# A fixed engine order for the first stage and the convolution of a hybrid recurrent/convolution decoder step, with later evictions and a gate pair moved to the end

## The chip, the cores and the metric

The kernel runs on one core of one Trainium2 chip. The metric is the device time in microseconds (us) of one execution; lower is better. A core has a matrix engine (PE, with its weight loads shown apart as PEld), a vector engine (DVE), an activation engine (ACT), a general engine (POOL) and a sync engine (SP), whose queue issues most DMAs. Each engine takes its own instructions in order and waits on semaphores for the others. [...]

## The reference, cut to what matters

One layer of a decoder: 16 learned meta tokens and 1,024 prompt tokens in one sequence, and 8 sequences of one token each ("samples") with a carried state. D_MODEL is 1,024.

```python
xn   = rmsnorm(h, norm_pre)
q, fr, i_in, z_a, b_g, c_g, h_c, z_b, gate_a, gate_b = split(xn @ w_in, 10)   # 1024 columns each
f    = lb + (1 - lb) * sigmoid(fr)                    # 8 heads of 128
S_t  = diag(f_t) S_{t-1} + (1 - f_t) i_t^T ;  o_t = silu(q_t)^T S_t
y_a  = (rmsnorm(o) * hgrn_norm * silu(z_a)) @ w_a
u    = c_g * h_c ;  conv = causal depthwise width-3 convolution of u
y_b  = (b_g * conv * silu(z_b)) @ w_b
out  = (sigmoid(gate_a) * y_a + sigmoid(gate_b) * y_b) @ w_o
h    = h + rmsnorm(out, norm_post)
```

It returns the prompt's and the samples' outputs, the new recurrent states and the new convolution contexts, all float32.

## The kernel before

Every float32 operand of a product is split into a high part (`fp32r`) and a low remainder, by `split`: a copy on ACT, then a subtraction on DVE or POOL. A product is three matmuls (`mm3`, lines 126 to 128).

**First stage.** Eight chunks of 128 tokens come in (even ones over SP's queue, odd ones in reversed order by an indirect DMA on POOL's queue). `prep_chunk` normalises a chunk (`normalise`: square with a row sum on ACT, inverse root on POOL, scaling on DVE at L186) and turns it (`turn`: four transposes on PE into a PSUM bank, high part on ACT, low part on DVE). The turned chunks are the column sets `b11, b21, b12, b22` of a two-by-two Strassen-like scheme with seven products; `sums12` and `sums34` (L207) form three more sets. Meanwhile `plain` computes the first head's `i` and `f` projections directly: four calls, each with 24 matmuls into one bank for `i` and 24 into another for `f`. Five masks for the recurrence (L82 to L88) are made at the very start.

**The stream.** `strassen` then computes all other projections in 39 pairs of sections. A pair has seven products (j = 0 to 6), each in two column chunks (c = 0, 1): 14 steps of 12 matmuls. In the step of product i, ACT makes the high part of the weights of product i + 2 (L687), DVE or POOL the low part (L693), and POOL the weight sums of the next pair (L673 to L675, L697). Right after its matmuls a step emits the eviction of its own output: for j = 0, 2, 4 a copy into a `held` tile (`sc`, L734), otherwise `evac`, which adds the held part (L270) and goes on with sigmoid and product. Some follow-up work goes into a list `later`, which `flush` empties in the next step.

**What is woven in.** `weave` spreads side work over the steps: the other turned sets over pair 0 (`later_sets`), then one head of the recurrence (`hgrn`) over every three pairs, then the eight samples' state updates (`sample_steps`) over the last fourteen pairs. Those pairs compute the convolution: `u_pair` forms u and its taps (L806, L808), `b_pair` multiplies by b and silu(z_b) (L828, L833, L834). Gate pairs (`gate_pair`) store sigmoid gates to DRAM; seven of them stand between the heads' pairs and the eighth stands right before the first `u_pair`. While the last pair runs, `fill` loads the heads' outputs back (`oz`, L925) and splits them.

**After the stream** `y_gemm` forms y_a and y_b (16 products of 96 matmuls each), the output projection follows, and the results are stored.

The order in which each engine gets its instructions is chosen by the scheduler of the language, by priorities in the order of the program and its own estimate of the times:

```python
for m in range(8):
    weave(stream, 42, hgrn(m), W_HG)
qz = slot("kt", 256)
pool.memset(qz, 0.0)
weave(stream, 14 * 14, sample_steps(), [1] * 64)
drain(stream)
context_out()
```

PSUM has two banks `ga`, two `gb` and four `h`. Weight operands (`w`) have three buffers, `sc` and `cs` two each. In odd pairs from number 25 on, a pair takes `h` banks in place of `ga`.

Of the kernel before, what the change touches and what calls it, by code (L numbers as in the profile page):

```python
# [19 lines left out]
HL = 524  # L20
# [12 lines left out]
def hybrid_step(ctx: ExitStack, tc: tile.TileContext,  # L33
# [46 lines left out]
    masks = const.tile([128, 5, 4, 128], U8, name="masks")  # L80
    pi, fi = slot("sc", 128, I32), slot("sc", 128, I32)
    pool.iota(pi[:, 0:128], pattern=[[0, 128]], base=0, channel_multiplier=1)  # L82
    pool.iota(fi[:, 0:128], pattern=[[1, 128]], base=0, channel_multiplier=0)
    for l in range(5):
        if l:
            for t in (pi, fi):
                vec.tensor_scalar(out=t[:, 0:128], in0=t[:, 0:128], scalar1=1, scalar2=None, op0=ALU.logical_shift_right)
        vec.tensor_tensor(out=masks[:, l], in0=cap(pi, 0, [[0, 4], [1, 128]]), in1=cap(fi, 0, [[0, 4], [1, 128]]),  # L88
                          op=ALU.is_equal)


# [71 lines left out]

    b11, b21, t2, b12, t3, t4, b22 = (factor(j) for j in range(7))
# [15 lines left out]
    def normalise(rows, xt):  # L180
        ms = small(1)
        act.activation(out=scratch[0:rows], in_=xt[0:rows, 0:1024], func=AF.Square, scale=1.0 / 32.0,
                       accum_out=ms[0:rows])
        rs = small(1)
        rsqrt(rs[0:rows], ms[0:rows])
        vec.scalar_tensor_tensor(out=xt[0:rows, 0:1024], in0=xt[0:rows, 0:1024], scalar=rs[0:rows, 0:1],  # L186
                                 in1=wpre[0:rows], op0=ALU.mult, op1=ALU.mult)

    def turn(xt, kk, to, c0):

        pt = hbank()
        for k in range(4):
            pe.transpose(pt[:, 128 * k:128 * k + 128], xt[:, 512 * kk + 128 * k:512 * kk + 128 * k + 128], ident)
        here = [[HL, 4], [1, 128]]
        split(cap(pt, 0, [[128, 4], [1, 128]]), cap(to[0], c0, here), cap(to[1], c0, here))

    def prep_chunk(c):
        xt = norm[c]
        normalise(128, xt)
        for kk in range(2):  # L200
            turn(xt, kk, ((b11, b12), (b21, b22))[kk][c % 2], 128 * (c // 2))
# [8 lines left out]
    def sums12(i, e1=None, e2=None):  # L210
        c = 2 * i
        less(block(c + 1, 0), block(c + 1, 0), block(c, 0), e1 or pool)
        less(block(c + 1, 1), block(c + 1, 1), block(c + 1, 0), e2 or vec)

    def sums34(i, e1=None, e2=None):
        c = 2 * i
        less(block(c, 0), block(c + 1, 1), block(c, 0), e1 or pool)
        less(block(c, 1), block(c, 1), block(c + 1, 1), e2 or pool)


    def load_small():
        xt = slot("k", 1024)
        sync.dma_start(xt[0:16, 0:1024], meta_tokens)
        sync.dma_start(xt[16:24, 0:1024], xs)
        return xt

    def prep_small(xt):

        normalise(24, xt)
        B = slot("sm", 192)  # L230
        for kk in range(2):
            pt = hbank()
            for k in range(4):
                c0 = 512 * kk + 128 * k
                pe.transpose(pt[:, 24 * k:24 * k + 24], xt[0:24, c0:c0 + 128], ident[0:24, 0:24])
# [18 lines left out]
    later = []  # L254

# [21 lines left out]

    def i_out(m, h, c0, n, pt, s):
# [6 lines left out]
    def f_out(m, h, c0, n, pt, s):  # L285
        out = of_head(m, "f", h, c0, n)
        sigmoid(added(pt, s, out), n, out)
        act.activation(out=out, in_=out, func=AF.Identity, scale=omlb[:, m:m + 1], bias=lb[:, m:m + 1])

    def q_out(m, h, c0, n, pt, s):  # L290
        out = of_head(m, "x", h, c0, n)
        y = added(pt, s)
        sg = sigmoid(y, n)
        later.append(lambda: (vec if s is None else pool).tensor_tensor(out=out, in0=y, in1=sg, op=ALU.mult))

    def z_out(m, h, c0, n, pt, s):
        out = of_head(m, "zs", h, c0, n)
        y = added(pt, s)
        sg = sigmoid(y, n)
        later.append(lambda: vec.scalar_tensor_tensor(out=out, in0=y, scalar=hnorm, in1=sg, op0=ALU.mult, op1=ALU.mult))  # L300
# [4 lines left out]
    def hgrn(m):  # L305
# [15 lines left out]
        turned(iT, V, 0)  # L321
# [7 lines left out]
        turned(iT, V, 1)  # L329
# [4 lines left out]
        ex = slot("ex", 24)  # L334
        pool.tensor_copy(cap(ex, 0, [[12, 2], [1, 12]]), cap(iT, 512, [[HL, 2], [1, 12]]))
# [192 lines left out]

    load_chunk(0)
    sync.dma_start(wpre, norm_pre.broadcast_to([128, 1024]))  # L530
    load_chunk(2)

    pv = slot("sm", 512)
    sync.dma_start(pv[0:16, 0:128], lb_logits.rearrange("j (m c) -> (j m) c", c=128))
    sync.dma_start(pv[16:40, 0:128], conv_w[0].rearrange("j (m c) -> (j m) c", c=128))
    sync.dma_start(pv[40:41, 0:128], hgrn_norm)
    pvp = hbank()
    pe.transpose(pvp[:, 0:41], pv[0:41, 0:128], ident[0:41, 0:41])
    vecs = const.tile([128, 41], F32, name="vecs")
    act.copy(vecs, pvp[:, 0:41])  # L540
    hnorm = vecs[:, 40:41]

    def tap(j, m):
        return vecs[:, 16 + 8 * j + m:17 + 8 * j + m]

    lbt = const.tile([128, 4, 8], F32, name="lbt")
    lb, omlb, mx, e1 = lbt[:, 0], lbt[:, 1], lbt[:, 2], lbt[:, 3]
    vec.tensor_tensor(out=mx, in0=vecs[:, 0:8], in1=vecs[:, 8:16], op=ALU.max)
    vec.tensor_tensor(out=lb, in0=vecs[:, 0:8], in1=mx, op=ALU.subtract)
    vec.tensor_tensor(out=e1, in0=vecs[:, 8:16], in1=mx, op=ALU.subtract)  # L550
    act.activation(out=lb, in_=lb, func=AF.Exp)
    act.activation(out=e1, in_=e1, func=AF.Exp)
    vec.tensor_tensor(out=e1, in0=e1, in1=lb, op=ALU.add)
    vec.reciprocal(out=e1, in_=e1)
    vec.tensor_tensor(out=lb, in0=lb, in1=e1, op=ALU.mult)
    vec.tensor_scalar(out=omlb, in0=lb, scalar1=-1.0, scalar2=1.0, op0=ALU.mult, op1=ALU.add)


    wp = (t4[0][:, 0:1024], t4[1][:, 0:1024])

    def plain(h, c0, n):

        banks = abank()[:, 0:n], bbank()[:, 0:n]
        for (wh, wl), pt in zip((wi, wf), banks):
            for k in range(8):
                xh, xl = at(((b11, b12), (b21, b22))[k // 4][h], k % 4)
                ks = slice(128 * k, 128 * k + 128)
                mm3(pt, wh[:, ks], wl[:, ks], xh[:, c0:c0 + n], xl[:, c0:c0 + n], k == 0, k == 7)

        def rest():  # L570
            for out, pt in zip((i_out, f_out), banks):
                out(0, h, c0, n, pt, None)
        return rest

    def part(to, which, i):
        turn(norm[2 * i + (which in (1, 2))], which in (2, 4), to, 128 * i)

    C0, C1 = chunks_of(HL)
    wi = weight(sec_of(2, 0), eng=pool)
    prep_chunk(0)  # L580
    load_chunk(1)
    prep_chunk(2)
    wf = weight(sec_of(1, 0), eng=pool, places=wp)
    load_chunk(3)
    for c in (4, 6):
        load_chunk(c)
    xsmall = load_small()
    for c in (5, 7):
        load_chunk(c)
    done = plain(0, *C0)  # L590
    prep_chunk(1)
    prep_chunk(3)
    done()
    done = plain(1, *C0)
    prep_chunk(4)
    prep_chunk(6)
    blocks = prep_small(xsmall)
    for b, to in zip(blocks, (b11, b12, b21, b22)):
        small_parts(b, to)
    done()  # L600
    sums12(0)
    sums12(1)
    part(t2, 2, 0)
    done = plain(0, *C1)
    prep_chunk(5)
    prep_chunk(7)
    s11, s12, s21, s22 = blocks
    for out, a, b, to in ((s12, s12, s11, None), (s22, s22, s12, t2), (s11, s22, s11, t3), (s21, s21, s22, None)):
        less(out, a, b, vec)
        if to:  # L610
            small_parts(out, to)
    done()
    part(t2, 2, 1)
    sums12(2)
    sums12(3)
    done = plain(1, *C1)
    part(t2, 2, 2)
    part(t2, 2, 3)
    for i in range(4):
        sums34(i)  # L620
    done()
    factors = [b11, b21, t2, b12, t3, t4, b22]

    def later_sets():

        part(b12, 1, 0)
        part(b12, 1, 1)
        small_parts(s12, b12)
        yield
        part(b12, 1, 2)  # L630
        part(b12, 1, 3)
        yield
        for i in range(4):
            part(t3, 3, i)
            if i % 2:
                yield
        small_parts(s21, t4)
        for i in range(4):
            part(t4, 4, i)
            if i % 2:  # L640
                yield
        cp = hbank()
        for h in range(2):
            cst = slot("sc", 512)
# [496 lines left out]
```

## Time and profile before

| | |
|---|---|
| time, median of 3 runs | 1313.67 us (1311.47 to 1315.06) |
| profiled execution | 1312.9 us, span 1311.1 us, mean granted clock 0.989 |
| PE busy | 1255.3 us (96%), 10,041 matmuls |
| DVE busy | 821.3 us (63%) |
| ACT busy | 538.0 us (41%) |
| POOL busy | 467.1 us (36%) |
| DMA | 117.12 MB, mean 89 GB/s |
| chain that ended last | PE 87%, POOL 5%, DVE 3%, DMA 2%, issue 2%, ACT 1% |

The span runs from the first to the last instruction; the profiled execution's own time is 1.8 us longer. "Granted clock" is the share of TensorE's full clock that the chip granted.

### The profile page before, as it was taken

Reading aid. Unit: us, or ns where it says so; the run is one execution under the profiler, and the core shown is the slowest. Engines: PE = TensorE matmul, PEld = TensorE weight load, DVE = VectorE, ACT = ScalarE, POOL = GpSimd, SP = SyncE. Lnnn points to the kernel's source line nnn. Section 1 sums busy time; section 2 is a strip of 40 time slices with the busy share of each in tenths; the row PEclk is TensorE's granted clock in tenths of the full one; section 3 lists DMA queues with packets and bytes.
Section 4 is the critical chain, followed back from the end, with each engine's and each line's share of the span. In section 5 each row is a group of like instructions: output and inputs, shape, how many; then the busy total and the mean of one; then the engine's idle time right before and its main releaser. Section 6 shows DMA issues by size and latency. Waiting matters only on the chain.

```text
span 1311.1 us, 25317 instructions
## 1 busy us (share of the span) xinstructions
PE 1255.3 (96%) x10041; PEld 1221.7 (93%) x10041; DVE 821.3 (63%) x1397; ACT 538.0 (41%) x1271; POOL 467.1 (36%) x530
## 2 busy tenths in 40 slices
PE   3799999999999999999999989989999999999997
PEld 3799999999999999999999889989999999999876
DVE  7558587785958678595876654755667623546052
ACT  5355555555555545555543333323334402313031
POOL 7555243333434333443344444653554000000010
PEclk9899999999999999999999999999999999999999
DMA  7011212121121212112214333332334633532041
GB/s 220 1 43 57 68 57 82 52 73 59 57 67 58 82 58 71 55 58 67 86 54 155 91 104 113 108 103 89 114 112 162 205 97 100 176 96 84 16 163 56
DMA packets 146533, 117.12 MB, mean 89 GB/s; under 512 B 6657, under 2 KB 130666, under 8 KB 146414
## 3 DMA queue, kind: packets, MB, share of 16 engines
q1 hardware_dynamic: 145838, 113.40, 27.7%
q0 software_dynamic: 576, 2.10, 0.5%
q8 instruction: 79, 1.29, 0.4%
q14 instruction: 40, 0.33, 0.1%
HBM read 89.48 MB, written 25.96 MB: 88 GB/s over the span
## 4 chain that ended last, share of the span: by engine, by line
PE 87%; POOL 5%; DVE 3%; DMA 2%; issue 2%; ACT 1%; DVEq 0%; SPq 0%; POOLq 0%; ACTq 0%
PE gb L126 10%; PE ga L127 10%; PE gb L127 10%; PE ga L126 10%; PE gb L128 10%; PE ga L128 10%; PE h L126 5%; PE h L128 5%; PE h L127 5%; PE h L413 3%; PE h L458 1%; PE h L318 1%; PE h L481 1%; PE h L479 1%; POOL ee L877 1%
## 5 line engine op out<-in xcount | busy, mean ns | idle before, releaser
L693 DVE TENSOR_TENSOR w<-wq,w 128x512 fp32r<-128x512 f32 x153 | 119.8, 783 | 68.3 <-ACT w L687 67.0
L687 ACT CAST w<-sm 128x512 fp32r<-128x512 f32 x117 | 72.3, 618 | 159.9 <-PE gb L128 128.3
L693 DVE TENSOR_TENSOR w<-sm,w 128x512 fp32r<-128x512 f32 x117 | 92.2, 788 | 36.5 <-ACT w L687 35.1
L734 ACT COPY sc<-ga 128x256 f32<-128x256 f32 x192 | 70.5, 371 | 89.3 <-PE ga L128 82.1
L1054 POOL TENSOR_TENSOR st<-st,half 128x1 f32<-128x1 f32 (+1 forms) x9 | 5.0, 551 | 279.3 <-DVE st L1052 276.4
L687 ACT CAST w<-wq 128x512 fp32r<-128x512 f32 x156 | 96.9, 621 | 16.8 <-PE h L128 13.2
L126 PE MATMUL gb<-s3h,w 128*128 128x256 f32 (+3 forms) x328 | 95.6, 291 | 6.5 <-DVE sc L270 5.7
L126 PE MATMUL gb<-s1h,w 128*128 128x256 f32 (+3 forms) x344 | 99.6, 290 | 0.0
L126 PE MATMUL gb<-s6h,w 128*128 128x256 f32 (+3 forms) x328 | 95.6, 292 | 1.6 <-DVE it L784 1.6
L127 PE MATMUL gb<-s1l,w 128*128 128x256 f32 (+3 forms) x344 | 97.2, 282 | 0.0
L127 PE MATMUL gb<-s6l,w 128*128 128x256 f32 (+3 forms) x328 | 93.7, 286 | 0.0
L127 PE MATMUL gb<-s3l,w 128*128 128x256 f32 (+3 forms) x328 | 93.7, 286 | 0.0
L128 PE MATMUL gb<-s3h,w 128*128 128x256 f32 (+3 forms) x312 | 89.2, 286 | 0.9 <-DVE w L693 0.9
L128 PE MATMUL gb<-s6h,w 128*128 128x256 f32 (+3 forms) x312 | 88.7, 284 | 0.0
L128 PE MATMUL gb<-s1h,w 128*128 128x256 f32 (+3 forms) x312 | 88.0, 282 | 0.0
L126 PE MATMUL ga<-s0h,w 128*128 128x256 f32 (+2 forms) x296 | 85.9, 290 | 0.0
L697 POOL TENSOR_TENSOR sm<-wq,sm 128x512 f32<-128x512 f32 x39 | 57.3, 1470 | 79.0 <-DVE w L693 58.7
L127 PE MATMUL ga<-s0l,w 128*128 128x256 f32 (+2 forms) x296 | 84.1, 284 | 0.6 <-DVE s0l L103 0.6
L126 PE MATMUL ga<-s5h,w 128*128 128x256 f32 (+3 forms) x256 | 74.5, 291 | 8.8 <-ACT sc L734 8.8
L126 PE MATMUL ga<-s2h,w 128*128 128x256 f32 (+3 forms) x272 | 79.8, 293 | 0.0
L675 POOL TENSOR_TENSOR sm<-wq 128x512 f32<-128x512 f32 x39 | 52.8, 1353 | 75.2 <-DVE w L693 74.3
L270 DVE TENSOR_TENSOR sc<-gb,sc 128x256 f32<-128x256 f32 (+1 forms) x144 | 60.4, 421 | 28.8 <-PE gb L128 16.7
(726 smaller groups left out, 4715.8 us busy)
## 6 DMA issues: line engine op xcount, KB each, us to landing
wq<-in_w_in_dram SPq DMA_DIRECT2D x160, 256.0 KB
oz<-zs SPq DMA_DIRECT2D x16, 258.0 KB
ob<-zs SPq DMA_DIRECT2D x8, 516.0 KB
x<-ga SPq DMA_DIRECT2D x8, 516.0 KB
x<-gb SPq DMA_DIRECT2D x8, 516.0 KB
ee<-vd SPq DMA_DIRECT2D x8, 512.0 KB
a<-in_state_hgrn_dram SPq DMA_DIRECT2D x8, 512.0 KB
out_dram<-a SPq DMA_DIRECT2D x8, 512.0 KB
```

The costliest lines, as they stand in the source:

```text
L126: pe.matmul(pt, wh, xh, start=first, stop=False, skip_group_check=onto)
L127: pe.matmul(pt, wh, xl, start=False, stop=False, skip_group_check=onto)
L128: pe.matmul(pt, wl, xh, start=False, stop=last, skip_group_check=onto)
L270: vec.tensor_tensor(out=out, in0=pt, in1=s, op=ALU.add)
L318: pe.transpose(pt[:, 128 * j:128 * j + 128], src[:, c0:c0 + 128], ident)
L413: pe.matmul(got[:, 128 * j:128 * j + 128], kms[:, ko + 128 * j:ko + 128 * j + 128], comp(X, 128 * j + B, nb // 4, HL - B, B), start=True, ...
L458: pe.matmul(pt[:, 128 * j:128 * j + 128], KT[:, 128 * i:128 * i + 128], V[:, 128 * i:128 * i + 128], start=True, stop=True)
L675: pool.tensor_tensor(out=s2, in0=a21, in1=a11, op=ALU.subtract)
L687: act.copy(w[:, 0:512], source(i))
L693: (pool if j in pairs[p][2] else vec).tensor_tensor(out=w[:, 512:1024], in0=source(i), in1=w[:, 0:512].bitcast(F32), op=ALU.subtract)
L697: pool.tensor_tensor(out=s2, in0=raws[p, 0, 1], in1=s2, op=ALU.subtract)
L734: act.copy(held[j][:, c0:c0 + n], o)
```

## The change

1. Two regions are put under `tc.manual_schedule()`, in which every engine issues its instructions in the order of the program: from the first loads to the end of pair 0, and from the samples' updates to `context_out`. The recurrence between them and all that follows stay with the scheduler.
2. The first stage is written out in an explicit order. Squares, scalings, transposes, high parts and low parts of the chunks are separate calls. Chunks 0, 1 and 3 are loaded first, then `wpre`, chunk 2 and the first weights. `plain` takes one weight at a time (24 matmuls). `sums12` is on DVE alone. The masks are made in the eighth slot of the work woven into pair 0, on DVE, with one shift for both index tiles.
3. In the fixed regions (`staged`), a step's eviction is not emitted in the step but put on `later`; the sigmoids after it go a step further, and the products another step.
4. Products of `q_out` and `b_pair` that were on POOL are on DVE. In the samples' update the product with the key moves from POOL to DVE, two small operations move from DVE to POOL and one to ACT; loads are issued one sample ahead into a second pair of tiles; the update has eleven slots in place of eight.
5. In `hgrn` both halves of V are turned in the first slot.
6. The eighth gate pair stands at the end of the stream, behind the convolution. The heads' outputs are loaded into eight tiles at the start of the last pair, and split one or two at a time over its first six products.

```diff
-    masks = const.tile([128, 5, 4, 128], U8, name="masks")
-    ... (iota, shifts and five comparisons at the start)
+    ordered = ExitStack()
+    ordered.enter_context(tc.manual_schedule())
...
+    def then(f):
+        if staged[0]:
+            later.append(f)
+        else:
+            f()
+    def silu(y, n, use, now=False):
+        def first():
+            sg = sigmoid(y, n)
+            later.append(lambda: use(sg))
+        first() if now else then(first)
...
     def q_out(m, h, c0, n, pt, s):
-        later.append(lambda: (vec if s is None else pool).tensor_tensor(out=out, in0=y, in1=sg, op=ALU.mult))
+        silu(y, n, lambda sg: vec.tensor_tensor(out=out, in0=y, in1=sg, op=ALU.mult), s is None)
...
-        turned(iT, V, 0)
+        for g in range(2):
+            turned(iT, V, g)
...
+        def after(j, c, c0, n, o, of_c, held, evac, end):
+            cols = slice(c0, c0 + n)
+            if j in (0, 2, 4):
+                act.copy(held[j][:, cols], o)
+            if j == 1:
+                evac(0, 0, c0, n, o, held[0][:, cols])
+            if j == 4:
+                then(lambda: evac(1, 1, c0, n, of_c[:, 0:n], held[4][:, cols]))
+            ...
                     (low if c else high)(i + 2)
-                    if j in (0, 2, 4):
-                        act.copy(held[j][:, c0:c0 + n], o)
-                    ...
+                    then(lambda a=(j, c, c0, n, o, pc[c] if j > 2 else None, held, evac, end): after(*a))
...
-    stream_of += [gates[7]] + [f(m) for m in range(8) for f in (u_pair, b_pair)]
+    stream_of += [f(m) for m in range(8) for f in (u_pair, b_pair)] + [gates[7]]
...
     b_pair:
-                (vec if h else pool).tensor_tensor(out=t, in0=t, in1=y, op=ALU.mult)
+                vec.tensor_tensor(out=t, in0=t, in1=y, op=ALU.mult)
-                    (pool if h else vec).tensor_tensor(out=sg, in0=y, in1=sg, op=ALU.mult)
+                    vec.tensor_tensor(out=sg, in0=y, in1=sg, op=ALU.mult)
...
     samples:
-        pool.tensor_tensor(out=cap(vb, 0, s3), in0=cap(vb, 0, s3), in1=over(3), op=ALU.mult)
+            vec.tensor_tensor(out=cap(vb, 0, s3), in0=cap(vb, 0, s3), in1=over(3), op=ALU.mult)
-        vec.tensor_copy(cap(qz, 0, [[33, 8]]), q)
+            pool.tensor_copy(cap(qz, 0, [[33, 8]]), q)
-        vec.tensor_scalar(out=so[:, 16:24], in0=pt[:, 0:8], scalar1=1.0 / 128.0, scalar2=None, op0=ALU.mult)
+            act.activation(out=so[:, 16:24], in_=pt[:, 0:8], func=AF.Copy, scale=1.0 / 128.0)
-        vec.tensor_tensor(out=smpz[:, 8 * m:8 * m + 8], in0=so[:, 8:16], in1=so[:, 16:24], op=ALU.mult)
+            pool.tensor_tensor(out=smpz[:, 8 * m:8 * m + 8], in0=so[:, 8:16], in1=so[:, 16:24], op=ALU.mult)
...
+    load_chunk(0); load_chunk(1); load_chunk(3); (wpre); load_chunk(2); (weights i)
+    square(0); load_chunk(5); load_chunk(7); square(2); normalise(0); turns(0); normalise(2)
+    highs(0); square(1); lows(0); turns(2); (weights i split); highs(2); normalise(1); lows(2)
+    square(3); (weights f split)
+    e1 = plain(wi, 0, *C0)
+    turns(1); normalise(3); highs(1); lows(1); square(4); turns(3); normalise(4); square(6); highs(3); lows(3)
+    e2 = plain(wf, 0, *C0)
+    turns(4); normalise(6); e1(); highs(4); lows(4); (lb from its logits: DVE, Exp on ACT, DVE); square("s", 24)
+    e1 = plain(wi, 1, *C0)
+    turns(6); normalise("s", 24); highs(6); lows(6); square(5); square(7); e2(); flush()
+    e2 = plain(wf, 1, *C0)
+    normalise(5); turn_small(); (small parts); normalise(7); turns(5); e1(); highs(5); lows(5)
+    e1 = plain(wi, 0, *C1)
+    turns(7); (small sums); e2(); flush(); highs(7); lows(7); sums12(0); sums12(1)
+    e2 = plain(wf, 0, *C1)
+    ... (sums12(2), sums12(3), first step of the stream's set-up, sums34 on POOL, two more plain calls)
+    weave(stream, 14, later_sets(), [1] * 9)
+    while later:
+        flush()
+    ordered.close()
+    staged[0] = False
     for m in range(8):
         weave(stream, 42, hgrn(m), W_HG)
+    staged[0] = True
+    ordered.enter_context(tc.manual_schedule())
-    weave(stream, 14 * 14, sample_steps(), [1] * 64)
+    weave(stream, 14 * 13 - 6, sample_steps(), [1] * (8 * N_SAMPLE))
     drain(stream)
     context_out()
+    ordered.close()
```

## Rows read from the trace of the kernel before

**Rows 1.** Windows by stage: us, busy us (instructions) by engine, clock, DMA, GB/s.
```profile
0.00:70.00 70.00, 40.72 (x287) 38.99 (x288) 41.39 (x65) 32.28 (x71) 46.58 (x55) 0.93 0.33 104
70.00:690.00 620.00, 620.00 (x5168) 615.13 (x5167) 458.14 (x724) 325.42 (x809) 249.79 (x290) 1.00 0.21 64
690.00:1005.00 315.00, 298.72 (x2508) 294.15 (x2507) 192.82 (x360) 109.86 (x253) 157.81 (x170) 0.98 0.36 110
1005.00:1030.00 25.00, 21.58 (x176) 20.55 (x174) 23.76 (x34) 18.98 (x30) 7.98 (x8) 1.00 0.82 269
```

**Rows 2.** Timeline of PE in the first stage: start, us, line, operands, [idle before <-releaser].
```profile
26.76 0.39 PE L127 MATMUL ga<-s0l,w 128*128 128x256 f32 x1 [0.63 <-DVE s0l L103]
...
40.54 0.58 PE L127 MATMUL ga<-s3l,w 128*128 128x256 f32 x1 [6.07 <-DVE s3l L103]
...
60.88 1.09 PE L193 MATMUL h<-ident,ee 128*128 128x128 f32 x4 [1.55 <-DVE s3l L103]
...
69.77 0.36 PE L127 MATMUL ga<-s0l,w 128*128 128x256 f32 x1
```

**Rows 3.** Windows at two pauses of the first stage: columns as before.
```profile
40.50:44.00 3.50, 3.46 (x17) 3.46 (x18) 2.49 (x4) 0.00 (x0) 3.50 (x3) 0.53 0.01 2
44.00:48.00 4.00, 4.00 (x37) 4.00 (x36) 0.00 (x0) 0.64 (x2) 1.47 (x2) 1.00 0.00 0
...
60.90:64.50 3.60, 3.60 (x18) 3.60 (x19) 3.50 (x6) 1.18 (x2) 2.33 (x3) 0.53 0.00 0
```

**Rows 4.** Timeline of ACT, DVE and POOL in the first 20 us.
```profile
4.23 1.06 ACT L182 ACTIVATE zs<-u 128x1024 f32<-128x1024 f32 x1 [1.91 <-DMA u<-in_x_prompt_dram]
...
6.53 1.32 DVE L186 SCALAR_TENSOR_TENSOR u<-u,st,x 128x1024 f32<-128x1024 f32 x1 [3.95 <-POOL st L95]
...
8.00 1.06 ACT L182 ACTIVATE zs<-s 128x1024 f32<-128x1024 f32 x1 [2.62 <-DMA s<-in_x_prompt_dram]
...
10.50 5.30 DVE L88 TENSOR_TENSOR masks<-sc 128x512 uint8<-128x512 int32 x1
...
18.55 0.68 DVE L103 TENSOR_TENSOR s0l<-h,s0h 128x512 fp32r<-128x512 f32 x1
...
20.09 0.67 DVE L88 TENSOR_TENSOR masks<-sc 128x512 uint8<-128x512 int32 x1
```

**Rows 5.** Timeline of POOL, DVE and ACT around 740 us.
```profile
737.02 1.90 POOL L877 TENSOR_TENSOR ee<-ee,smpv 128x1024 f32<-128x1024 f32 x1
...
738.96 2.29 DVE L879 TENSOR_TENSOR a<-a,ee 128x1024 f32<-128x1024 f32 x1 [3.75 <-POOL ee L877]
...
743.81 0.17 DVE L902 TENSOR_TENSOR smpz<-so 128x8 f32<-128x8 f32 x1 [1.89 <-POOL so L95]
...
744.95 0.42 ACT L275 ACTIVATE cs<-sc 128x256 f32<-128x256 f32 x1 [5.19 <-DVE sc L270]
```

**Rows 6.** Waits of PE and DVE, 690 to 1030 us: total, times, longest.
```profile
PE ga L126 <- ACT sc L734: 8.8, 3, 4.8
...
DVE a L879 <- POOL ee L877: 17.7, 6, 4.4
DVE smpz L902 <- POOL so L95: 16.8, 8, 3.3
```

**Rows 7.** Windows of lowered clock in the convolution: columns as before.
```profile
740.00:750.00 10.00, 6.74 (x43) 6.33 (x42) 5.63 (x13) 2.64 (x7) 5.15 (x6) 0.85 0.34 102
...
780.00:793.00 13.00, 9.38 (x56) 9.17 (x55) 8.15 (x14) 2.96 (x7) 7.88 (x8) 0.74 0.22 62
...
880.00:890.00 10.00, 5.19 (x32) 4.99 (x31) 5.58 (x10) 2.15 (x6) 5.46 (x6) 0.84 0.19 58
```

**Rows 8.** Groups of instructions, 701 to 1005 us: count, busy, mean ns, idle before.
```profile
L875 DVE TENSOR_TENSOR a<-a,smpv 128x1024 f32<-128x1024 f32 x8 | 10.2, 1278 | 7.2 <-DMA a<-in_state_hgrn_dram 7.2
...
L833 DVE TENSOR_TENSOR cs<-ga,cs 128x256 f32<-128x256 f32 x7 | 2.9, 417 | 0.0
```

**Rows 9.** Chain of waits at 1,001 us: start, us, what.
```profile
1001.71 3.16 DMA it<-oz
```

More of the change, by code (lines that the diff above doesn't have):

```diff
@@ L575, in part @@
[L575 to L611, printed above, removed]
@@ L708, in strassen @@
             held = {}
+            if p == len(pairs) - 1:
+                tail["load"]()
             for j in range(7):
@@ new lines, in hybrid_step @@
+    square(0)
+    load_chunk(5)
+    load_chunk(7)
+    square(2)
+    normalise(0)
+    turns(0)
+    normalise(2)
+    highs(0)
+    square(1)
+    lows(0)
+    turns(2)
+    for kk in range(2):
+        w_high(ri, wi, kk)
+        w_low(ri, wi, kk)
+    highs(2)
+    normalise(1)
+    lows(2)
+    square(3)
+    for kk in range(2):
+        w_high(rf, wf, kk)
+        w_low(rf, wf, kk)
+    e1 = plain(wi, 0, *C0)
+    turns(1)
+    normalise(3)
+    highs(1)
+    lows(1)
+    square(4)
+    turns(3)
@@ new lines, in hybrid_step, with tap @@
+    normalise(4)
+    square(6)
+    highs(3)
+    lows(3)
+    e2 = plain(wf, 0, *C0)
+    turns(4)
+    normalise(6)
+    e1()
+    highs(4)
+    lows(4)
+    pvp = hbank()
+    pe.transpose(pvp[:, 0:41], pv[0:41, 0:128], ident[0:41, 0:41])
+    vecs = const.tile([128, 41], F32, name="vecs")
+    act.copy(vecs, pvp[:, 0:41])
+    hnorm = vecs[:, 40:41]
+    def tap(j, m):
+        return vecs[:, 16 + 8 * j + m:17 + 8 * j + m]
+    lbt = const.tile([128, 4, 8], F32, name="lbt")
+    lb, omlb, mx, e1 = lbt[:, 0], lbt[:, 1], lbt[:, 2], lbt[:, 3]
@@ new lines, in hybrid_step @@
+    square("s", 24)
+    e1 = plain(wi, 1, *C0)
+    turns(6)
+    normalise("s", 24)
+    highs(6)
+    lows(6)
+    square(5)
+    square(7)
+    e2()
+    flush()
+    e2 = plain(wf, 1, *C0)
+    normalise(5)
+    s11, s12, s21, s22 = turn_small()
+    for b, to in ((s11, b11), (s12, b12), (s21, b21), (s22, b22)):
+        small_parts(b, to)
+    normalise(7)
+    turns(5)
+    e1()
+    highs(5)
+    lows(5)
+    e1 = plain(wi, 0, *C1)
+    turns(7)
+    for out, a, b in ((s12, s12, s11), (s22, s22, s12), (s11, s22, s11), (s21, s21, s22)):
+        less(out, a, b, vec)
@@ new lines, in hybrid_step @@
+    small_parts(s22, t2)
+    e2()
+    flush()
+    highs(7)
+    lows(7)
+    for i in range(2):
+        sums12(i)
+    e2 = plain(wf, 0, *C1)
+    turn(1, 1)
+    turn(3, 1)
+    for i in range(2, 4):
+        sums12(i)
+    next(stream)
+    for c in (1, 3):
+        turn_high(c, 1, t2)
+        turn_low(c, 1, t2)
+    e1()
+    for i in range(4):
+        sums34(i)
+    e1 = plain(wi, 1, *C1)
+    e2()
+    flush()
+    turn(5, 1)
+    turn(7, 1)
+    e2 = plain(wf, 1, *C1)
+    for c in (5, 7):
+        turn_high(c, 1, t2)
+        turn_low(c, 1, t2)
```

380 lines of the change are left out of this document (202 added, 178 removed).

## The prediction

> **What bounds the kernel now.** First the windows by stage [rows 1]. From 70 to 690 us, the recurrence, PE is busy in all 620 us at the full clock: 5,168 instructions in 620 us, 0.12 us each, so a step of 12 matmuls is 1.44 us. Nothing there can be gained by order alone. PE's idle time lies elsewhere: 29.3 us before 70 us (70 less 40.7), 16.3 us in the convolution (315 less 298.7), 3.4 us in the last pair (25 less 21.6). What an order can give back is there.
>
> Second, PE's timeline in the first stage [rows 2]: the first long run of projections starts at 26.76 us, there is a pause of 6.07 us before 40.54 and one of 1.55 us before 60.88, and pair 0 of the stream runs from 69.77. After each pause the clock is lower: 17 matmuls in the 3.5 us after 40.5 at a granted 0.53, against 37 in the next 4 us at 1.00 [rows 3]. At full speed the 17 take 2.0 us, so such a phase loses about 1.5 us.
>
> Third, what the pauses in the convolution wait for [rows 5, 6]. PE waits for ACT's copy into `sc` (8.8 us, three times). Behind that stands a row of engines: DVE waits 3.75 us for POOL's key product (L877), later 1.89 us for POOL's power (L95), so its addition into `sc` is late, so ACT's sigmoid waits 5.19 us, and the copy that PE needs stands behind that sigmoid. Over the stretch DVE waits 17.7 us for L877 and 16.8 us for L95. After the three longest pauses the clock is lower [rows 7]: 10 us at 0.85, 13 at 0.74, 10 at 0.84, a loss of 1.5 + 3.4 + 1.6 = 6.5 us of clock time, some 0.7 of it while PE stood still anyway.
>
> **The first stage, part by part.** The sum is made against the profiled execution's 1312.9 us; the median of the runs is 1313.67, so nothing separates the two.
>
> *Start.* Before, DVE is held by a mask comparison for 5.30 us at 10.50, and by another later; the first low part comes only at 18.55 though its chunk was ready to be scaled at 6.53 [rows 4]. The change takes the masks away from there. What bounds the start then is loads: chunk 0 releases ACT at 4.23 and chunk 2, with the norm weights between them, at 8.00 [rows 4], so 1.05 MB in 3.77 us, 278 GB/s. Now chunks 1 and 3 go on POOL's queue at once and share that rate. Chunk 2 lands at 8.0 if they take nothing, at 4.23 + 2.1 MB / 278 = 11.8 if they go wholly before it; I take 10.0. From chunk 0's square to its scaling were 2.3 us (4.23 to 6.53), so chunk 2 is scaled from 12.3 to 13.6. Behind that, in DVE's fixed order, stand the low parts of chunk 0 (two at 0.6 to 0.68), the scaling of chunk 1 (1.25) and the low parts of chunk 2: 3.7 us, so the projections start at 17.3, bounds 15 and 20. That is 9.5 us earlier than 26.76.
>
> *From there to pair 0.* Before, this took 43.0 us (26.76 to 69.77), with pauses of 6.07 and 1.55 and about 1.2 in small ones, and two slow phases of 1.5. Work is left of about 31 us, and by count the same: 192 projection matmuls at 0.12 (23.0) and some 70 transposes at about 0.12. With the durations of rows 4 I laid the new order out by hand. DVE has 25 us of work in this stretch, so it doesn't bound it as a sum, but PE still waits four times: 1.9 us before the small block's transposes (their scaling waits for a square that stands on ACT behind the two exponentials, and those wait for DVE), 1.8 us for chunk 5, 1.2 us for the small low parts, 1.2 us for `sums12`. With 2 us for one slow phase this makes 31 + 6 + 2 = 39 us, so pair 0 starts near 56.5, 13 us earlier. Bounds: 16 if the pauses go, 4 if half of the early start is lost to waits for chunks 4 and 6, which land last.
>
> *The masks* now stand in DVE's order after the twelfth step of pair 0. Five comparisons at 0.67 [rows 4] and four shifts, put at 0.5, are 5.4 us. Queued behind them is the product that frees pair 0's PSUM bank, which pair 1 needs two steps (2.9 us) on; PE waits about 2.5 us. Nothing if DVE gets there early; 8 us if a comparison lasts 5.30 again, as it did beside POOL's reading. I take 3. The first stage gives -13 + 3 = **-10**, from -16 to +4.
>
> **The recurrence.** `q_out` puts two products of 0.42 us per head on DVE, which is busy 458 of 620 us [rows 1]: hidden. The transposes of V come earlier, not more often. Other pairs stand beside head 7, and PE is already full: 0. Above, a per cent of new pauses would be 6 us.
>
> **Start of the second region.** The second convolution tile uses the slot of head 7's gated output, and with the gate pair gone from in front its first tap now comes in the very first steps of the region, on ACT, before that output has been stored. Comparable: a 516 KB load took 3.16 us from issue to landing [rows 9]. With the last product of the recurrence about 1.5 us into the region, ACT's first tap can start some 5 us in, 3.5 us later than its turn, and behind it in ACT's fixed order stand weight casts and copies with about 2 us of slack. I take **+2** (0 to 5).
>
> **The convolution.** The two waits of DVE for POOL in each sample vanish, since the key product is on DVE and the last product on POOL. DVE gets eight products of about 1.28 us (that of L875) and 24 of 0.42 (L833) [rows 8], some 20 us: 193 [rows 1] + 20 = 213 of about 300 us, 71%, and a few small operations leave it. Evictions come one step later, so each PSUM bank is held 1.44 us longer. The tightest: the copy of product 4 must be done within one step, and ACT has nothing before it there that waits for DVE; the addition into the bank of product 6 has two steps, 2.9 us, on a queue that holds at most a sample's 1.28, a low part's 0.68 [rows 4] and two additions of 0.42. Loads come one sample ahead, 22 steps or 32 us, against the single microseconds of a load. So most of 16.3 + 5.8 = 22 us comes back; I leave 4 us for bursts: **-18**, from -22 to -8.
>
> **The last pair.** Its loads are now issued before it, not in step with its splits, and nothing of taps and b products is left beside them. DVE was busy 23.8 of 25 us there [rows 1]; now it has seven low parts, six additions and eight subtractions, 7 x 0.68 + 6 x 0.42 + 8 x 1.28 = 17.5 of 20. Of 3.4 us I take **-2** (0 to -3). The work after it is unchanged.
>
> **Sum.** 1312.9 - 10 + 0 + 2 - 18 - 2 = 1284.9, **1285 us**.
>
> **Rivals.**
>
> *A. The clock takes back part of the first stage.* Four pauses of 1.2 to 1.9 us now stand where there was one of 6, and even 1.55 us was followed by a phase at 0.53 [rows 2, 3]. If each brings 3.5 us of half speed, that is 4 x 1.5 = 6 us where the sum has 2, and with the start at its late bound of 20 us, 1285 + 4 + 3 = 1292. For it: rows 3. Against it: DVE, not PE, sets part of this stretch, so a slower PE costs less than its whole loss. The Trainium skill, page "TensorE: Matmul & The Clock Gate", section "HAM oscillation — how this bites in real kernels", says that repeated pauses make the array fall back to the slow clock each time, and each burst after them starts slow; by that rule this rival would be the rule. The trace agrees for its two pauses, at 0.53.
>
> *B. The fixed order gives back half of the convolution.* The scheduler's order let other work pass a late instruction; a fixed one does not. If POOL's weight sums and power are late, ACT's taps wait, and casts behind them. At 0.7 us for each of 14 pairs, 10 us are lost: 1295. For it: ACT's wait of 5.19 us for DVE [rows 5] shows what a blocked queue does. Against it: the wait that started that row is removed.
>
> *C. Slower.* One mechanism: the addition that frees the bank of product 6 comes late in every pair of the second region, because evictions start one step later. Slack is 2.9 us; from 2 us more than that per pair (14 pairs, 28 us) the gain is gone, at 3.5 us the time is 1312.9 - 28 + 49 = 1334. For it: bursts on DVE of several products. Against it: DVE has 71% of work, and a burst of 4.9 us in each pair is not in the list of its instructions.
>
> *D. No change.* The pauses are set by something that stays, POOL's own sum of work or the loads, and merely show at another wait: 1310 to 1315. Against it: POOL was busy half of the convolution (158 of 315 us [rows 1]) and loses work.
>
> **How the numbers follow.** Chances: forecast (1277 to 1290) 0.5; better than that, pauses nearly gone, 0.1; A 0.14; B and mixtures of A and B up to 1308, 0.14; D 0.04; C 0.08. The range leaves out C, D and the ends: 1272 (first stage -16, convolution -22, last pair -3, boundary 0) to 1302 (A and B together, 1285 + 7 + 10). About 0.3%, 4 us, is what a measurement of this kernel can tell from no change. Faster 0.87, same 0.04, slower 0.09.
>
> **What would show it.** In the changed trace: projections from about 17 us, pair 0 from 56 to 57 us, a DVE block of masks near 75 us with a PE pause behind it; no wait of DVE for L877's or L95's successors; PE idle in the convolution at 4 us with clock 1.00; an ACT wait for a store at the region's start. The prediction is wrong if PE pauses once per pair in the second region, if the recurrence no longer shows PE at 100%, or if pair 0 starts after 65 us.

## The result, and the profile after

| | before | after |
|---|---|---|
| median of 4 runs each, same chip | 1312.57 us | 1290.45 us (1289.68 to 1291.45) |
| ratio, 95% interval | | 0.9831 [0.981, 0.9851] |
| profiled execution | 1312.9 us, span 1311.1 | 1289.68 us, span 1287.9 |
| mean granted clock | 0.989 | 0.997 |

The change makes the kernel 22 us faster (1290.45 us). That is inside the range of 1272 to 1302 us. The forecast was 1285 us: the gain is some 5 us smaller than its sum.

First the windows by stage of the kernel after (columns as in [rows 1]).

```profile
0.00:70.00 70.00, 51.44 (x359) 48.90 (x360) 46.22 (x65) 38.11 (x85) 42.73 (x55) 0.95 0.36 115
70.00:690.00 620.00, 614.36 (x5115) 608.56 (x5115) 471.77 (x772) 318.28 (x794) 212.71 (x239) 1.00 0.20 62
690.00:1005.00 315.00, 309.27 (x2646) 303.91 (x2645) 228.06 (x390) 126.42 (x293) 135.75 (x167) 1.00 0.42 132
```

Against [rows 1], PE is idle 18.6 us in the first 70 us (29.3 before), 5.6 us in the recurrence (nothing before) and 5.7 us in the convolution (16.3 before); there the granted clock is 1.00 where it was 0.98. Two of the three stages give back, one takes. Of the 5.6 us, 3.7 still belong to pairs 0 and 1 (before 115 us) and 1.9 to pairs 22 to 24.

The stages move against each other, so a ruler that moves with the work is better: the start of a pair of the stream, which is PE's first matmul with `s0` of that pair. All starts below are read from PE's timeline of the profiled execution, in us.

| | before | after | the two lengths up to the next line |
|---|---|---|---|
| pair 0 starts | 69.77 | 61.01 | 25.92, 29.07 |
| pair 1 | 95.69 | 90.08 | 532.98, 533.83 |
| pair 22 (beside head 7's end) | 628.67 | 623.91 | 76.30, 78.38 |
| pair 25 (beside the samples) | 704.97 | 702.29 | 294.67, 277.65 |
| pair 38, the last | 999.64 | 979.94 | 24.86, 21.95 |
| end of the stream | 1024.50 | 1001.89 | 288.4, 287.8 to the end |

So the 23.2 us of the two profiled executions are -8.8 + 3.1 + 0.9 + 2.1 - 17.0 - 2.9 - 0.6. Three quarters come from the convolution. The numbers count positions in the stream. With the eighth gate pair at the end, each position from 22 on holds in the kernel after the pair that stood one later before: positions 25 to 37 are six u pairs and seven b pairs where they were seven and six, and position 38 is a gate pair where it was a b pair.

The two engines' waits from 690 to 1030 us in the kernel after (total, times, longest). DVE's two largest and PE's two largest:

```profile
DVE w L611 <- ACT w L605: 21.5, 17, 2.7
DVE zs L718 <- ACT zs L716: 13.6, 7, 2.0
...
PE gb L114 <- DVE sc L288: 2.5, 2, 1.7
PE gb L116 <- DVE w L611: 1.7, 4, 0.5
```

DVE's 17.7 and 16.8 us for POOL [rows 6] are gone from the list. What DVE waits for now costs PE little: PE's own longest entries are 2.5 and 1.7 us, where it waited 8.8 us for ACT's copies alone.

### The profile page after: what moved, and what is told of

It reads as the page before. It is cut to its first block, busy times and chain, and to the rows that moved or that the text cites. A ratio compares the mean times of both kernels' runs of the same rounds, so it can differ in the third digit from the quotient of the medians.

```text
span 1287.9 us, 25281 instructions
## 1 busy us (share of the span) xinstructions
PE 1251.0 (97%) x10041; PEld 1216.1 (94%) x10041; DVE 852.9 (66%) x1444; ACT 536.7 (42%) x1280; POOL 396.1 (31%) x470
## 3 DMA queue, kind: packets, MB, share of 16 engines
q8 instruction: 79, 1.29, 0.4%
## 5 line engine op out<-in xcount | busy, mean ns | idle before, releaser
L611 DVE TENSOR_TENSOR w<-wq,w 128x512 fp32r<-128x512 f32 x153 | 129.7, 847 | 57.7 <-ACT w L605 56.7
L591 POOL TENSOR_TENSOR sm<-wq 128x512 f32<-128x512 f32 x39 | 67.1, 1721 | 166.1 <-DVE w L611 151.7
L611 DVE TENSOR_TENSOR w<-sm,w 128x512 fp32r<-128x512 f32 x117 | 87.0, 743 | 30.1 <-ACT w L605 29.6
L615 POOL TENSOR_TENSOR sm<-wq,sm 128x512 f32<-128x512 f32 x39 | 60.3, 1545 | 123.1 <-DVE w L611 94.4
L114 PE MATMUL ga<-s0h,w 128*128 128x256 f32 (+3 forms) x288 | 83.2, 289 | 1.1 <-DVE zs L327 1.1
L115 PE MATMUL ga<-s0l,w 128*128 128x256 f32 (+3 forms) x288 | 81.2, 282 | 0.0
L593 POOL TENSOR_TENSOR sm<-wq 128x512 f32<-128x512 f32 x39 | 55.5, 1423 | 70.7 <-DVE w L611 67.9
```

What stands on the lines that cost most here:

```text
L114: pe.matmul(pt, wh, xh, start=first, stop=False, skip_group_check=onto)
L115: pe.matmul(pt, wh, xl, start=False, stop=False, skip_group_check=onto)
L591: pool.tensor_tensor(out=s3, in0=a11, in1=a21, op=ALU.subtract)
L593: pool.tensor_tensor(out=s2, in0=a21, in1=a11, op=ALU.subtract)
L611: (pool if j in pairs[p][2] else vec).tensor_tensor(out=w[:, 512:1024], in0=source(i), in1=w[:, 0:512].bitcast(F32), op=ALU.subtract)
L615: pool.tensor_tensor(out=s2, in0=raws[p, 0, 1], in1=s2, op=ALU.subtract)
```

## The experiments

For the convolution there were two theories. **W**: the gain is the waits of DVE for POOL in the samples' update, which go because operations change engine; the fixed order has no part in it. **O**: it is the order, with evictions in three steps, and the moves are a side matter. For the first stage the question was why pair 0 starts 4.5 us later than predicted. The differences of medians below are against the 1290.45 us of the kernel after; the median of the kernel before lay between 1312.57 and 1314.1 us in the groups of runs, so differences of 1.5 us between groups mean nothing by themselves. Intervals are of the ratio to the kernel before.

### The moves alone, in the kernel before

```diff
  b_pair, in the kernel before
-                (vec if h else pool).tensor_tensor(out=t, in0=t, in1=y, op=ALU.mult)
+                vec.tensor_tensor(out=t, in0=t, in1=y, op=ALU.mult)
-                    (pool if h else vec).tensor_tensor(out=sg, in0=y, in1=sg, op=ALU.mult)
+                    vec.tensor_tensor(out=sg, in0=y, in1=sg, op=ALU.mult)
  samples
-        pool.tensor_tensor(out=cap(vb, 0, s3), in0=cap(vb, 0, s3), in1=over(3), op=ALU.mult)
+        vec.tensor_tensor(out=cap(vb, 0, s3), in0=cap(vb, 0, s3), in1=over(3), op=ALU.mult)
-        vec.tensor_copy(cap(qz, 0, [[33, 8]]), q)
+        pool.tensor_copy(cap(qz, 0, [[33, 8]]), q)
-        vec.tensor_scalar(out=so[:, 16:24], in0=pt[:, 0:8], scalar1=1.0 / 128.0, scalar2=None, op0=ALU.mult)
+        act.activation(out=so[:, 16:24], in_=pt[:, 0:8], func=AF.Copy, scale=1.0 / 128.0)
-        vec.tensor_tensor(out=smpz[:, 8 * m:8 * m + 8], in0=so[:, 8:16], in1=so[:, 16:24], op=ALU.mult)
+        pool.tensor_tensor(out=smpz[:, 8 * m:8 * m + 8], in0=so[:, 8:16], in1=so[:, 16:24], op=ALU.mult)
```

> The kernel before, under the scheduler as it was, with only the engine moves of the convolution: the samples' key product and the b products on DVE, the last small products on POOL and ACT. Theory W (the gain of the convolution comes from taking away DVE's waits for POOL): about 1299 us, 12 to 16 under the kernel before, no wait of DVE for the key product or for the power. Theory O (it comes from the fixed order and the later evictions): 1309 to 1313 us.

Measured: 1291.49 us, 0.9823 [0.9806, 0.984]. Six lines, with the scheduler's order everywhere and no later evictions, give the gain of the whole change within the measurement. Pair 0 still starts at 70.29 us; pairs 25 to 37 take 273.66 us, 21.0 less than in the kernel before and 4.0 less than in the kernel after. The time lies below W's 1299 us: the moves are worth more than W had said. O falls, and W holds in its cause.

### The samples' operations back on their old engines, in the kernel after

The four `samples` lines of the diff above, reversed, in the kernel after (its b products stay on DVE).

> The changed kernel with the samples' four operations back on the engines they had before, in the fixed order. Theory W: 1302 to 1306 us, 12 to 16 more than the changed kernel, and DVE again waits for POOL's key product and power. Theory O: 1290 to 1293 us.

Measured: 1297.76 us, 0.9876 [0.9857, 0.9895]: 7.3 us slower than the kernel after, between the ranges of the two theories. Of DVE's two waits for POOL only the one for the power is back (first line, from 700 to 980 us). The sum behind the key product (L804 here) no longer waits for POOL. PE waits for the low part of the weights and for an addition (the two lines behind it):

```profile
DVE smpz L829 <- POOL so L83: 15.5, 7, 2.6
...
PE gb L116 <- DVE w L611: 5.4, 6, 1.9
PE gb L114 <- DVE sc L288: 3.8, 2, 2.1
```

So in the kernel after, the four moves are worth 7.3 us. In the kernel before, the three small operations alone, with which the wait for the power goes, are worth 17.1 us (next section). The wait itself is as long in both (16.8 us before, 17.6 us here, from 690 to 1030 us). Later evictions are meant to take up a late DVE in this way, but the kernel after also loads a sample ahead and spreads a sample over eleven slots, and no run separates the three.

### One move at a time, in the kernel before

Of the diff of the first experiment: the key product alone (`over(3)`); the three small operations alone; the two b products alone.

> The kernel before with one edit: the samples' key product on DVE in place of POOL. All moves together gave 1291.5 us, 22 less than before. If the three groups of moves add up by the waits that they take away (17.7 us for the key product, 16.8 for the power, 16.5 for the b products): about a third, 1304 to 1308 us. If POOL's load was the cause and any relief frees the rest: 1293 to 1298 us.

> The kernel before with one edit: the samples' last small products on POOL and ACT, so that DVE no longer waits for the power, while the key product stays on POOL. If the waits add up: 1304 to 1308 us. If only POOL's load matters, which this edit doesn't lower: 1311 to 1315 us.

> The kernel before with one edit: all products of the b pairs on DVE. If the waits add up: 1306 to 1310 us. If POOL's load was the cause: 1295 to 1303 us.

| | median, us | ratio [95%] | pairs 25 to 37, us |
|---|---|---|---|
| key product | 1305.1 | 0.9939 [0.9917, 0.9962] | 284.55 |
| three small operations | 1296.96 | 0.9871 [0.9851, 0.9891] | 278.18 |
| two b products | 1311.6 | 0.9983 [0.997, 0.9996] | 292.11 |

Against their 1314.1 us of before that is 9.0, 17.1 and 2.5 us; together 28.6, more than the 22 of all at once, so the gains overlap. Only the first run came out as one of its two expectations said (1304 to 1308 us). The small operations gave more than either expectation for them, the b products less than either. The largest part is three operations on at most 128x8 elements. Waits from 690 to 1030 us, of the first two:

```profile
DVE smpz L902 <- POOL so L95: 17.7, 8, 3.3
PE ga L126 <- ACT sc L734: 5.7, 3, 2.9
```

```profile
DVE a L879 <- POOL ee L877: 17.4, 6, 4.4
PE ga L126 <- ACT sc L734: 3.9, 4, 1.8
```

With the small operations moved, DVE still waits 17.4 us for the key product, as long as before [rows 6], and yet 17 of 22 us are gained. The two waits of DVE are equally long (17.7 and 16.8 us) but not equally dear. Why the one for the power is dearer, no run shows. What the traces show is that a long wait can be cheap. In the kernel after, POOL waits in DVE's place, for ACT's small results in front of the power (690 to 1030 us). In sum that is longer than either wait was on DVE, and PE has no wait for POOL in this stretch:

```profile
POOL so L82 <- ACT so L827: 29.8, 6, 6.6
```

### The scheduler's order in one region, or in both

```diff
  scheduler's order from the samples on
     staged[0] = True
-    ordered.enter_context(tc.manual_schedule())
  scheduler's order in the first stage
     ordered = ExitStack()
-    ordered.enter_context(tc.manual_schedule())
```

> The changed kernel with the scheduler's order in the second region; the program's order, the later evictions and the engine moves stay. Theory W: 1290 to 1294 us, PE idle in the convolution near 5 us as in the changed kernel. Theory O: 1303 us or more.

> The changed kernel with the scheduler's order in the first region; the order in which the program is written stays. If the written order and the masks' move make the first stage's gain: 1289 to 1293 us, pair 0 near 61 us. If it is the fixing of the order: pair 0 at 66 us or later and 1294 to 1300 us.

> The changed kernel with no fixed order anywhere; program order, later evictions, engine moves and the gate pair's place stay. If the two freed regions add up (4.6 and 2.5 us less than the changed kernel): 1282 to 1285 us, faster than both kernels and than the kernel before with the moves alone (1291.5). If the end of pair 0 eats the first region's part: 1285 to 1287 us.

| | median, us | ratio [95%] | pair 0 | pair 2 | pairs 25 to 37 |
|---|---|---|---|---|---|
| after | 1290.45 | 0.9831 [0.981, 0.9851] | 61.01 | 114.76 | 277.65 |
| free from the samples on | 1285.82 | 0.9785 [0.9769, 0.9802] | 59.38 | 113.43 | 274.35 |
| free in the first stage | 1287.95 | 0.9804 [0.9791, 0.9818] | 62.55 | 111.37 | 277.65 |
| free in both | 1283.18 | 0.9764 [0.975, 0.9778] | 62.68 | 111.49 | 274.13 |

All else of the change is kept: the program's order, its loads, the later evictions, the moves. Without any fixed order it is the fastest version, 7.3 us below the kernel after and 2.4% below the one before, as the two freed regions added up had promised. Each region alone came out a little below what was expected for it (1285.82 for 1290 to 1294 us, 1287.95 for 1289 to 1293 us). In the convolution the fixed order costs 3 to 4 us (277.65 against 274.13); in the first stage it makes pair 0 start 1.5 us sooner (61.01 against 62.55), and yet pair 2 starts 3.4 us later (114.76 against 111.37).

### Fixed order, with evictions in their own step again

```diff
-    staged[0] = True
     ordered.enter_context(tc.manual_schedule())
```

> The changed kernel with fixed order in the second region, but evictions emitted in their own step as in the kernel before. Theory W: 1290 to 1295 us. Theory O: 1300 us or more, with PE waiting for copies or additions into sc in every pair, since in a fixed order an eviction that waits for the step just issued holds the weight casts behind it.

Measured: 1301.42 us, 0.9902 [0.9885, 0.9919], 11 us slower than the kernel after; pairs 25 to 37 take 287.70 us. The time is in O's range, but the sign that O named does not show: PE waits for the low part of the weights, not for copies or additions into `sc`. Waits from 700 to 980 us:

```profile
PE h L116 <- DVE w L611: 10.2, 7, 3.4
ACT zs L716 <- POOL x L705: 32.0, 7, 5.7
```

ACT's first tap waits in its fixed row for POOL's copies inside u (7 times, 32.0 us in this run, 12.8 in the kernel after). At PE's longest wait the timeline shows the rest: DVE's taps wait 2.0 us for ACT's, the low part of the weights stands behind them, and PE waits 3.40 us for it. So the later evictions are what makes a fixed order bearable there; they are not what made the kernel faster.

### The first stage: DVE and POOL apart

In the kernel after, DVE forms eight differences (`sums12`) while POOL forms the weight sums and `sums34`. One edit puts the last `sums34` call in front of the stream's set-up, so that POOL's work of that moment stands behind its wait for DVE's differences.

```diff
+    sums34(3)
     ...                      # next(stream): the first weights and their sums
-    for i in range(4):
+    for i in range(3):
         sums34(i)
```

> The changed kernel with one pair of POOL's differences put first, so that POOL waits until DVE's eight differences of the first stage are done instead of working beside them. Theory P (the two engines hold each other up when both read two operands from SBUF: each difference took 1.65 to 1.75 us beside POOL, 0.68 alone): DVE's differences end near 50 instead of 57 us, the PE pause of 2.7 us and most of the one of 1.5 us go, and the slow clock after them, pair 0 starts at 55 to 57.5 us, time 1285 to 1288 us. Rival Q (the pauses come from the order itself, with the small block and the last chunks late): pair 0 at 60 to 62 us, time 1289 to 1292 us. Under P a later PE wait for the turned differences of pair 0 may give some of it back.

Measured: 1288.43 us, 0.981 [0.9796, 0.9824]. DVE and POOL on the timeline in the kernel after (start, us, engine, line):

```profile
45.00 0.68 DVE L219 TENSOR_TENSOR a<-a,u 128x512 f32<-128x512 f32 x1
...
47.28 1.75 DVE L219 TENSOR_TENSOR ee<-ee,s 128x512 f32<-128x512 f32 x1
49.07 1.63 DVE L219 TENSOR_TENSOR ee<-ee 128x512 f32<-128x512 f32 x1
50.63 1.75 DVE L219 TENSOR_TENSOR v<-v,kt 128x512 f32<-128x512 f32 x1
...
46.78 1.71 POOL L591 TENSOR_TENSOR sm<-wq 128x512 f32<-128x512 f32 x1
...
51.80 1.72 POOL L219 TENSOR_TENSOR u<-a,u 128x512 f32<-128x512 f32 x1
...
60.23 1.30 POOL L219 TENSOR_TENSOR kt<-kt,v 128x512 f32<-128x512 f32 x1
```

and in the experiment:

```profile
47.04 0.68 DVE L219 TENSOR_TENSOR ee<-ee,s 128x512 f32<-128x512 f32 x1
...
48.37 0.69 DVE L219 TENSOR_TENSOR v<-v,kt 128x512 f32<-128x512 f32 x1
...
54.07 1.29 POOL L611 TENSOR_TENSOR w<-wq,w 128x512 fp32r<-128x512 f32 x1
...
55.88 0.28 PE L114 MATMUL ga<-s0h,w 128*128 128x256 f32 x1
...
71.45 0.39 PE L116 MATMUL gb<-s3h,w 128*128 128x256 f32 x1 [2.79 <-POOL w L611]
```

The same operation takes DVE 0.68 us alone and 1.63 to 1.75 beside POOL, and POOL 1.3 alone and some 1.7 beside DVE. The Trainium skill, page "SBUF — State Buffer", section "SBUF: two separate sides", says that a VectorE operation with two SBUF inputs and a GpSimd operation that reads SBUF take one port pair in turn, each for its whole instruction. The trace agrees in kind but not in size: in turns, 0.69 and 1.3 us would make a pair every 2.0 us, and DVE's operations here follow each other at 1.6 to 1.8.

With the engines apart PE's two pauses for DVE's differences, 4.25 us in the kernel after, are down to 0.70, and pair 0 starts at 55.88 us, as P said. Q falls. The slow phase of the clock does not go, as P had it; it comes earlier (shown further below). And what POOL had done meanwhile is now late: PE waits 2.79 us for the low part of the weights in pair 0, and pair 2 starts only 1.8 us earlier than in the kernel after. Of 5.1 us at pair 0, 2 are left at the end, in the medians hardly more than groups of runs differ by; the time lies just above P's range.

### The masks at the very start

The block that makes the five masks moves from the eighth slot of pair 0 to behind the first three loads; its index tile comes from `sc` in place of `k`.

> The changed kernel with the masks made at the very start, where DVE has nothing to do until 6.6 us. If the masks in pair 0 cost what was predicted: 2 to 4 us less, 1287 to 1289 us, with no DVE block of 5 us in pair 0. Rival: beside POOL's indirect loads the comparisons or the loads are held up, chunk 1 lands later, and the first projections start after 17 us: 1290 to 1293 us.

> Both: the differences apart and the masks first. If the two gains add: 1282 to 1286 us. If what is gained ahead of pair 0 is lost again when the recurrence starts (DVE is full there): 1287 to 1290 us.

Measured: 1289.55 us, 0.9817 [0.9804, 0.9831] with the masks alone; 1286.16 us, 0.9789 [0.9776, 0.9802] with the masks and the edit of `sums34`. Timeline of DVE in the run with the masks alone:

```profile
4.86 0.69 DVE L902 TENSOR_TENSOR masks<-sc 128x512 uint8<-128x512 int32 x1 [4.86 <-POOL sc L897]
...
9.69 1.28 DVE L183 SCALAR_TENSOR_TENSOR u<-u,st,x 128x1024 f32<-128x1024 f32 x1
```

DVE is free up to 4.86 us, but the index tile is not there: POOL has issued its indirect loads first. So the scaling of chunk 0 comes at 9.69 instead of 6.63 us, and pair 0 starts 2.2 us later (63.18). Pairs 0 and 1 together are 3.6 us shorter than in the kernel after (50.19 against 53.75), so 1.4 are left at pair 2, and 0.9 in the medians, which by itself couldn't be told from nothing. The time lies between the two expectations, and each has its part: pair 0 is rid of the masks, and the start is held up as the rival had it, though by the masks themselves and not by a late chunk. With `sums34` moved too, pair 2 starts at 109.87 us, 4.9 us earlier than in the kernel after, and 4.3 us of it are left at the end (1286.16 us, between the two ranges).

## Why the prediction was right, and where it was off

**The convolution: right, -17.0 us for a sum of -18 and +2.** The reason named for it, the two waits of DVE in each sample, is shown by the moves alone and, for the power, from the other side by the run that takes the samples' moves back. What the prediction did not see is that most of it hangs on three small operations (17.1 of 22 us in the kernel before): it took the two waits as one. That the number agrees so well is in part luck. The moves alone give -21.0 us in these pairs, close to the whole 22 us that it had to win, and the fixed order takes 3 to 4 of them back, about as much as it had set aside for bursts.

**The first stage: the term that was mis-sized, -5.6 us measured for -10** (-8.8 at pair 0, +3.1 in it). Its start came out at 16.07 us for 17.3. PE's timeline in the kernel after, and ACT's before it:

```profile
7.92 1.06 ACT L176 ACTIVATE zs<-s 128x1024 f32<-128x1024 f32 x1 [2.57 <-DMA s<-in_x_prompt_dram]
...
14.91 0.62 ACT L909 CAST s4h<-wq 128x512 fp32r<-128x512 f32 x1 [2.63 <-DMA wq<-in_w_in_dram]
16.07 0.58 PE L114 MATMUL ga<-s0h,s4h 128*128 128x256 f32 x1 [2.68 <-ACT s0h L196]
...
47.51 0.63 PE L192 MATMUL h<-ident,a 128*128 128x128 f32 x4 [1.53 <-DVE a L219]
...
50.85 1.08 PE L192 MATMUL h<-ident,ee 128*128 128x128 f32 x4 [2.72 <-DVE ee L219]
```

Chunk 2 landed by 7.92 us, not 10.0; the first weights came last, and ACT waited 2.63 us for them. So the size was near and the last link another. What failed is the step from there to pair 0: 39 us predicted (31 of work, 6 of pauses, 2 for a slow phase), 44.9 measured. It laid out DVE's work with the durations of [rows 4], 0.68 us an operation, and put 1.2 us for the wait at `sums12`. There, PE paused 1.53 and 2.72 us, since the differences took 1.63 to 1.75 us beside POOL, and a slow phase followed (columns as in [rows 1]):

```profile
51.50:57.00 5.50, 5.50 (x27) 5.50 (x26) 5.43 (x4) 1.78 (x4) 5.50 (x5) 0.51 0.02 4
```

27 matmuls in 5.5 us at 0.51 of the clock, 0.20 us each where [rows 3] has 37 in 4 us: 2.6 us lost.

The whole stretch up to pair 0, in the kernel after and then in the run with DVE and POOL apart:

```profile
16.07:61.01 44.94, 38.51 (x265) 36.77 (x266) 35.29 (x49) 24.59 (x57) 26.57 (x25) 0.92 0.20 55
16.20:55.88 39.68, 36.81 (x266) 35.23 (x266) 27.77 (x49) 24.08 (x56) 15.72 (x19) 0.96 0.21 58
```

In the kernel after PE is idle for 6.4 us, about the 6 of the sum: the pauses at `sums12` are 3 us longer than forecast, and the others together nearly as much shorter. The excess is in busy time, 38.5 us for 31 + 2. The slow phase lost 2.6 us, and the first 24 matmuls, at 0.23 us each (last section), some 2.6 against 0.12. That leaves 33.3 us, which the sum put at 31. With the engines apart the predicted start of pair 0 is met within 0.6 us, but by other terms, 2.9 us idle and 36.8 busy, so this is in part luck. A slow phase is there too, only earlier. The same stretch of time in that run and in the kernel after:

```profile
39.00:43.00 4.00, 4.00 (x21) 4.00 (x21) 3.31 (x9) 2.19 (x6) 0.00 (x0) 0.57 0.00 0
39.00:43.00 4.00, 4.00 (x34) 3.99 (x34) 3.54 (x11) 2.19 (x7) 0.00 (x0) 1.00 0.00 0
```

In both runs PE has waited 1.29 us for chunk 5 before this (at 37 us). In one the clock falls, in the other it does not. So a pause of this length alone doesn't tell whether a slow phase follows, and why it came in one run only stays open.

**The masks: right in size, over two pairs.** Forecast +3; by the run that moves them they cost 3.6 us, 1.6 in pair 0 and 2.0 in pair 1. That pair 0 as a whole became 3.1 us longer is a coincidence, since it also holds more transposes than before (17 more instructions of PE) and two waits of 1.0 us together that stay when the masks go. These are the waits of PE that go with the masks:

```profile
90.08 0.39 PE L114 MATMUL ga<-s0h,w 128*128 128x256 f32 x1 [0.40 <-DVE zs L327]
92.51 0.39 PE L114 MATMUL ga<-s0h,w 128*128 128x268 f32 x1 [0.74 <-DVE zs L327]
111.73 0.39 PE L114 MATMUL gb<-s6h,w 128*128 128x256 f32 x1 [1.56 <-DVE f L288]
```

The first two are the wait that the prediction named, for the products that free pair 0's banks: 1.1 us for 2.5. The third, late in pair 1, was not forecast.

**The recurrence: 0 forecast, +2.9 measured.** Pairs 1 to 21 take 0.9 us more, less than pair 1 alone (24.68 us for 23.19), where the masks' delay still shows. Pairs 22 to 24 take 2.1 us more. PE's timeline there in the kernel after:

```profile
655.73 1.16 PE L440 MATMUL h<-x,u 128*128 128x128 f32 x8 [1.04 <-DVE x L448]
...
662.10 1.13 PE L440 MATMUL h<-x,u 128*128 128x128 f32 x8 [0.90 <-DVE x L448]
```

These two waits are the loss: PE had 0.1 us of idle time there before, 1.9 after. "Other pairs stand beside head 7" was counted as nothing because PE was full; but a pair of u has more on DVE than the gate pair it replaces (63.4 us of DVE work in pairs 22 to 24 for 60.5), and head 7 waits for DVE. It is not the fixed order: without any, the three pairs take 77.72 us, and with only the engine moves in the kernel before 75.98. One of the prediction's own signs of being wrong, PE below 100% in the recurrence, is met in these three pairs and in pair 1; from pair 2 to pair 21 PE is busy throughout. Whether the gate pair's move or the earlier transposes of V are behind it wasn't tried apart and stays open.

**The region's start: +2 forecast.** ACT did wait at its first tap, 4.68 us, but for POOL's copies inside u:

```profile
704.07 0.72 ACT L716 ACTIVATE zs<-x,vecs 128x512 f32<-128x512 f32 x1 [4.68 <-POOL x L705]
```

The wait for the store that the prediction named does not show. PE was idle 0.8 us from 702.3 to 724.4 us. The reason was wrong and the price smaller.

**The last pair: -2.9 for -2.** With only the engine moves in the kernel before it stays at 24.57 us (24.86 before), so this part does belong to the new end of the stream, though not to its fixed order: without any it takes 21.01 us. Whether the loads or the other pair at this place matter more wasn't tried.

**The rivals.** A came near in size: the slow matmuls cost some 5.2 us where it named 6 and the sum had 2. A slow phase after each pause did not come: after the 1.29 us for chunk 5 the clock stayed. B, that a fixed order gives back part of the convolution, is true in its kind: 3 to 4 us of pairs 25 to 37 and 4.6 in the medians, where it named 10. The prediction's sum had no term for it. C did not come: the addition that frees product 6's bank is not late, as PE's longest wait in the region is 1.7 us. D falls with the starts of pairs 0 and 25 to 38.

The sum against the measured terms: first stage 4.4 us worse than forecast, recurrence 2.9 worse, region's start and convolution together 1.0 better, last pair 0.9 better, the rest 0.6 better; 4.8 us in all, which is 1289.7 for 1284.9.

## What to carry to other kernels

A tiny operation on an in-order engine that waits for another engine can hold up everything queued behind it: move the waiting end to the engine that it waits for, and do not price a wait by its length: taking away two equally long ones gave 9.0 and 17.1 us here. Try such moves alone before an order is written out by hand; here six lines gave what the whole rewriting gave, and the rewritten program ran fastest with the scheduler left on. When an order is laid out by hand with durations from a trace, look at what the neighbour engine does at that moment in the new order.

## What the runs showed of the hardware that was not expected

The size of the loss when DVE and POOL work side by side: 0.69 us became 1.63 to 1.75 on DVE, 1.3 became some 1.7 on POOL.

And a stretch at the start where the granted clock doesn't fit the matmuls (columns as in [rows 1], kernel after):

```profile
15.90:21.70 5.80, 5.48 (x24) 5.19 (x24) 3.58 (x3) 2.68 (x6) 4.96 (x5) 1.00 1.11 313
```

24 matmuls are busy for 5.48 us, 0.23 us each, about the pace of the 27 at 0.51 above, while the column says 1.00. Before them PE had only turned two chunks, and had stood idle for 2.68 us. From one start to the next are 0.21 us for 256 columns, and in the stretch at 0.51 it is 0.22 for 268: the same per column. That speaks for a low clock before its first recorded change. In the kernel before, the first long run (26.76 us) comes behind 4 us of almost unbroken work, mostly transposes, and goes at 0.12 us each. Whether it was the clock or something else that slowed these matmuls, no run here settles.
